# An encoder's MLP: pairs of up-projection tiles as seven products of blocks in place of eight

## The chip, the core and the metric

The kernel runs on one core of one Trainium2 chip. The metric is the device time of one execution in microseconds (us), as the median of several runs. The engines are named as in the profile: PE (TensorE; PEld is its weight load), DVE (VectorE), ACT (ScalarE), POOL (GpSimd) and SP (SyncE, which here only issues DMAs).

## What is computed

A bidirectional encoder of two layers, width 1024, runs over a prompt of 512 tokens and a sample of 256 with the same weights, 768 tokens in all. Each layer is an attention block with four kinds of heads and then this MLP:

```
def conv_gated_mlp(x, w_up, b_up, conv_w, conv_b, w_down):
    h = x @ w_up + b_up                      # 1024 -> 5632
    hp = jnp.pad(h, ((0, 0), (CONV_W // 2, CONV_W // 2), (0, 0)))
    h = conv_w[0] * hp[:, :-2] + conv_w[1] * hp[:, 1:-1] + conv_w[2] * hp[:, 2:] + conv_b
    a, b = jnp.split(h, 2, axis=-1)
    return (jax.nn.silu(a) * b) @ w_down     # 2816 -> 1024

...
x = x + conv_gated_mlp(rms_norm(x, g_ffn[l]), w_up[l], b_up[l], conv_w[l], conv_b[l], w_down[l])
```

All inputs and outputs are float32.

## The kernel before, in words

Activations are kept transposed: eight tiles of 128 features by 768 tokens. TensorE takes a rounded format (fp32r), so every factor is split into a high part, which ACT copies, and a low part, which `lo` (line 147) subtracts on POOL or DVE. `acc3` (lines 174 to 184) makes each product from three matmuls: high by high (L180), high by low (L182), low by high (L183). A matmul takes a 128x128 block of weights and up to 512 token columns; the prompt and the sample go separately, with 512 and 256 columns.

`weights` (from line 154) loads a block of weights by SP's queue into `wraw` (two buffers), makes `wh` on ACT (L158) and `wl` in halves of 512 columns on POOL (L147). `wh` and `wl` have four buffers of 1024 columns each.

The MLP (`mlp`, from line 1117) goes over 22 feature tiles i. For each i, `up` computes columns i and 22 + i of the up projection: 8 x 3 matmuls with 512 columns into a `mm` bank of PSUM and 8 x 3 with 256 into a `pt` bank (two banks of each). ACT adds the bias and writes `hb` (L1140), where the prompt and the sample lie with zeros around them. `conv` is one pass on ACT (L1147) and two on DVE (L1149, L1150) over 769 columns. Then come silu on ACT (L1163), the product of the halves on DVE (L1164), and its split into `gh` (ACT, L1167) and `gl` (DVE). The down projection (`down`) takes chunks of 8, 7 and 7 feature tiles. It stands on PE behind the first up tiles of the next chunk: per chunk eight output tiles, each with the prompt into a `sc` bank (two) and the sample into the `o` bank (one), and DVE adds each result to x (L1196).

Every engine works its list in order. The tile framework decides that order when the program is built, and it also inserts the waits on buffers.

Of the kernel before, what the change touches and what calls it, by code (L numbers as in the profile page):

```python
# [9 lines left out]
F32 = mybir.dt.float32  # L10
# [17 lines left out]
CHUNKS = ((0, 8), (8, 15), (15, 22))  # L28
# [18 lines left out]
RING, TMP_BUFS, P_BUFS, PT_BUFS, GH_BUFS = 32, 3, 9, 2, 9  # L47
# [8 lines left out]
       "rbc": "d", "pl": "d", "cmb": "d"}  # L56
WHOLD, DHOLD = (1, 3), (6, 7)
# [25 lines left out]
def encoder(ctx: ExitStack, tc, a, y):  # L83
# [11 lines left out]
    con = cp.tile([P, NCON], F32, name="con")  # L95
# [58 lines left out]
    def weights(src, n):  # L154
        raw = load_weights(src, n)
# [6 lines left out]
        return h, l  # L162

    def small_weights(src, n):
        raw = wp.tile([P, 1024], F32, tag="wraw", bufs=2, name="uraw")
        nc.sync.dma_start(out=raw[:, :n], in_=src)
        h = wp.tile([P, 256], F32R, tag="uh", bufs=2, name="uh")
        l = wp.tile([P, 256], F32R, tag="ul", bufs=2, name="ul")
        act.activation(h[:, :n], raw[:, :n], AF.Copy)
        lo(eng("ul"), l[:, :n], raw[:, :n], h[:, :n])  # L170
        return h, l
# [103 lines left out]
    def attention(l, x, par, sm, xin, loads, ready):  # L275
        lam_init = 0.8 - 0.6 * math.exp(-0.3 * l)


# [49 lines left out]
        def new_v(nm):  # L328
            return new_v1(nm + "0") + new_v1(nm + "1")

# [168 lines left out]
        class AHead:  # L499
# [7 lines left out]
            def first(self, si):  # L507
# [7 lines left out]
                for i in range(nt):  # L515
                    k0, k1 = max(0, i - 1) * P, min(nt, i + 2) * P
                    w = k1 - k0
                    p = pq[:, i * n:(i + 1) * n] if si else p_tile()[:, :w]
                    u = k0 - (i - 1) * P
                    jobs.append((mms, off + i * P, off + k0, w, p, con[:, C_AT + u:C_AT + u + w]))  # L520
                    probs.append((p, k0, w))
# [120 lines left out]
        def b_rope_k(kr):  # L642
# [3 lines left out]
            kc = con[:, C_KC:C_KC + 128].rearrange("p (t d) -> p t d", t=4)  # L646
            ks = con[:, C_KS:C_KS + 128].rearrange("p (t d) -> p t d", t=4)
# [101 lines left out]
        class DHead:  # L749
# [7 lines left out]
            def first(self, si):  # L757
# [5 lines left out]
                for g in range(0, nt, 2):  # L763
                    jobs = []
                    for m in range(2):
                        for i in (g, g + 1):
                            u = 384 - i * P
                            p = pq[m][:, i * n:(i + 1) * n] if si else p_tile()
                            jobs.append(([(self.st["q", m], self.st["k", m])], off + i * P, off, n, p,
                                         con[:, C_DT + u:C_DT + u + n]))  # L770
# [206 lines left out]
        if not xin:  # L977
            nc.sync.dma_start(out=con[:, C_AT:], in_=a["con"][:, C_AT:])
# [139 lines left out]
    def mlp(l, x, par, mp, u, ready):  # L1118
# [8 lines left out]

        def up(col, si):
            if col not in tiles:
                tiles[col] = upw(col)  # L1130
                hb = mp.tile([P, T + 3], F32, tag="hb", bufs=3, name="hb")
                bufs[col] = hb
                for c in (0, TP + 1, T + 2):
                    pool.memset(hb[:, c:c + 1], 0.0)
# [8 lines left out]
        def conv(col):  # L1143
            hb = bufs[col]
            t = mp.tile([P, T + 1], F32, tag="cv", bufs=4, name="cv")
# [9 lines left out]
        seq += [(c, si) for i in range(2, FT) for c in (i, FT + i) for si in (0, 1)]  # L1155

        def ff(i):
            while seq and not (i in tiles and FT + i in tiles and (i, 0) not in seq and (i, 1) not in seq
                               and (FT + i, 0) not in seq and (FT + i, 1) not in seq):
                up(*seq.pop(0))  # L1160
            ta = conv(i)
# [3 lines left out]
            gh = mp.tile([P, T], F32R, tag="gh", bufs=GH_BUFS, name="gh")  # L1165
            gl = slot("gl")
            act.activation(gh[:, :TP], ta[:, :TP], AF.Copy)  # L1167
            act.activation(gh[:, TP:], ta[:, TP + 1:], AF.Copy)
            lo(dve, gl[:, :TP], ta[:, :TP], gh[:, :TP])
            lo(dve, gl[:, TP:], ta[:, TP + 1:], gh[:, TP:])  # L1170
            return gh, gl

        def down(gs, f0, f1):
            last = f1 == FT
            order = [(m, si) for m in range(KT) for si in (0, 1)]
            if last:
                a0, b0 = (1, 0) if l < L - 1 else (0, 1)
                order = [(m, si) for m in range(5) for si in (0, 1)]
                order += [(m, si) for si in (a0, b0) for m in (5, 6, 7)]
            ws, count = {}, [0]  # L1180
            nf = f1 - f0
            for m, si in order:
                if m not in ws:
                    ws[m] = weights(a["w_down"][l, m, :, f0 * P:f1 * P], nf * P)
# [5 lines left out]
                else:  # L1190
                    out = b_sc() if si == 0 else b_o()
                i = acc3(out[:, :n], [((wh[:, i * P:(i + 1) * P], wl[:, i * P:(i + 1) * P]),
                                       (gs[i][0][:, off:off + n], gs[i][1][:, off:off + n])) for i in range(nf)])
                if last and si == b0 and m in DHOLD:
                    behind(i, marks[DHOLD.index(m)])
                dve.tensor_tensor(x[m][:, off:off + n], out[:, :n], x[m][:, off:off + n], op=ALU.add)  # L1196
                if last:
                    xsquare(x, m, si)
                    if (m, si) == (KT - 1, a0):
                        nxt.extend(ready(x))  # L1200

        nxt = []
        pending = None
        for f0, f1 in CHUNKS:
            gs = []
            for i in range(f0, f1):
                gs.append(ff(i))
                if pending is not None:
                    down(*pending)
                    pending = None  # L1210
            pending = (gs, f0, f1)
# [162 lines left out]
```

## Time and profile before

| | |
|---|---|
| median of three runs | 1946.84 us (1944.7 to 1950.02) |
| the profiled execution, its own time | 1950.42 us |
| its span, first to last instruction | 1948.5 us |
| granted TensorE clock, mean | 0.983 |
| PE / PEld busy | 96% / 84% of the span |
| DVE / ACT / POOL busy | 54% / 47% / 38% |
| first layer's MLP | about 433 to 950 us |
| second layer's MLP | about 1400 to 1948 us |

The profile gives for each engine its busy time, for each group of instructions its count, mean duration and the idle time of its engine ahead of it, and for each instruction its start. Matmuls are pipelined: a matmul's duration is longer than the distance to the next one's start, and that distance is what the engine spends on it.

### The profile page before, as it was taken

The page shows a single profiled execution, that of the slowest core. Times are in us where ns is not written, and L with a number is a line of the kernel's source. Part 1 is how long each engine was busy: PE and PEld are TensorE (multiplying, and loading weights), DVE is VectorE, ACT ScalarE, POOL GpSimd, SP SyncE. Part 2 cuts the span into 40 slices and gives each one's busy share as a digit, 9 for nine tenths or more (in the row PEclk, how much of TensorE's full clock was granted, in tenths as well). Part 3 has the DMA queues.
Part 4 walks back from the last instruction along what each step waited for, and adds up shares of the span by engine and source line. Part 5 has one row for each costly group of instructions (what it writes and reads, how often), then busy time and mean ns, then how long its engine had stood idle before and what let it go on. Part 6 is the DMA issues. An engine that isn't in the chain of part 4 may idle for free.

```text
span 1948.5 us, 28713 instructions
## 1 busy us (share of the span) xinstructions
PE 1876.7 (96%) x10932; PEld 1636.4 (84%) x10932; DVE 1042.9 (54%) x1875; ACT 914.7 (47%) x1776; POOL 736.1 (38%) x937
## 2 busy tenths in 40 slices
PE   8899998999999999999999999999999999999997
PEld 6778886888888888888978888778888888888886
DVE  5688779746442244134356877894554314432443
ACT  4466667545442244144335766773454314422441
POOL 1325536354333233333343363643543333323331
PEclk8899999999999999999999999999999999999998
DMA  4322005021222222221334110141122221122211
GB/s 171 91 62 75 26 12 147 26 73 56 71 57 64 66 65 58 63 67 59 115 96 127 50 43 17 47 122 54 56 75 65 65 65 58 58 69 66 63 57 65
DMA packets 46297, 133.64 MB, mean 69 GB/s; under 512 B 6736, under 2 KB 10704, under 8 KB 46160
## 3 DMA queue, kind: packets, MB, share of 16 engines
q1 hardware_dynamic: 45872, 131.56, 23.0%
q8 instruction: 86, 1.41, 0.3%
q14 instruction: 51, 0.42, 0.1%
q10 hardware_dynamic: 288, 0.26, 0.0%
HBM read 109.77 MB, written 6.29 MB: 60 GB/s over the span
## 4 chain that ended last, share of the span: by engine, by line
PE 82%; DVE 9%; ACT 3%; POOL 2%; issue 1%; DMA 1%; SPq 0%; DVEq 0%; ACTq 0%; POOLq 0%
PE mm L180 14%; PE mm L182 13%; PE mm L183 13%; PE pt L182 6%; PE pt L183 6%; PE pt L180 6%; PE sc L180 4%; PE sc L183 3%; PE sc L182 3%; PE sc L399 2%; PE o L378 2%; PE pt L370 2%; PE o L183 1%; PE o L180 1%; PE o L182 1%
## 5 line engine op out<-in xcount | busy, mean ns | idle before, releaser
L147 POOL TENSOR_TENSOR wl<-wraw,wh 128x512 fp32r<-128x512 f32 (+3 forms) x377 | 477.2, 1288 | 611.3 <-ACT wh L158 556.7
L158 ACT ACTIVATE wh<-wraw 128x1024 fp32r<-128x1024 f32 (+3 forms) x188 | 190.7, 1015 | 373.3 <-PE o L183 110.8
L1149 DVE SCALAR_TENSOR_TENSOR cv<-hb,par,cv 128x769 f32<-128x769 f32 x88 | 161.0, 1831 | 358.7 <-ACT cv L1147 358.7
L182 PE MATMUL mm<-ul,wh 128*128 128x512 f32 x704 | 275.2, 391 | 0.7 <-POOL ul L147 0.4
L180 PE MATMUL mm<-uh,wh 128*128 128x512 f32 x704 | 274.1, 391 | 0.1
L183 PE MATMUL mm<-uh,wl 128*128 128x512 f32 x704 | 273.9, 389 | 0.0
L182 PE MATMUL pt<-ul,wh 128*128 128x256 f32 x704 | 200.5, 285 | 1.5 <-POOL ul L147 1.4
L180 PE MATMUL pt<-uh,wh 128*128 128x256 f32 x704 | 199.8, 284 | 1.7 <-ACT wh L158 1.0
L183 PE MATMUL pt<-uh,wl 128*128 128x256 f32 x704 | 199.7, 284 | 0.0
L343 POOL TENSOR_SCALAR p<-p,s 128x512 f32<-128x512 f32 (+2 forms) x160 | 103.2, 659 | 217.9 <-DVE s L772 103.4
L183 PEld LDWEIGHTS mm<-uh,wl 128*128 128x128 f32 x704 | 132.2, 188 | 28.1
L182 PEld LDWEIGHTS mm<-ul,wh 128*128 128x128 f32 x704 | 132.5, 188 | 25.9 <-POOL ul L147 0.8
L180 PEld LDWEIGHTS mm<-uh,wh 128*128 128x128 f32 x704 | 132.3, 188 | 25.8 <-ACT hb L1140 0.6
L180 PEld LDWEIGHTS pt<-uh,wh 128*128 128x128 f32 x704 | 135.3, 192 | 6.2 <-ACT wh L158 1.8
L182 PEld LDWEIGHTS pt<-ul,wh 128*128 128x128 f32 x704 | 135.5, 192 | 5.8 <-POOL ul L147 1.9
L183 PEld LDWEIGHTS pt<-uh,wl 128*128 128x128 f32 x704 | 135.5, 192 | 0.2
L180 PE MATMUL mm<-xh,wh 128*128 128x256 f32 (+1 forms) x360 | 126.2, 353 | 2.3 <-DVE dl L147 1.7
L182 PE MATMUL mm<-xl,wh 128*128 128x256 f32 (+1 forms) x360 | 125.4, 349 | 0.9 <-DVE xl L147 0.9
L183 PE MATMUL mm<-xh,wl 128*128 128x256 f32 (+1 forms) x360 | 125.3, 349 | 0.0
L180 PE MATMUL sc<-gh,wh 128*128 128x512 f32 (+1 forms) x324 | 122.9, 379 | 0.0
L183 PE MATMUL sc<-gh,wl 128*128 128x512 f32 (+1 forms) x324 | 122.2, 377 | 0.0
L182 PE MATMUL sc<-gl,wh 128*128 128x512 f32 (+1 forms) x324 | 121.4, 375 | 0.0
(299 smaller groups left out, 4470.2 us busy)
## 6 DMA issues: line engine op xcount, KB each, us to landing
wraw<-w_up SPq DMA_DIRECT2D x88, 512.0 KB, 3.6
wraw<-w_down SPq DMA_DIRECT2D x32, 448.0 KB, 3.3
wraw<-w_in SPq DMA_DIRECT2D x26, 512.0 KB, 3.7
wraw<-w_down SPq DMA_DIRECT2D x16, 512.0 KB, 3.6
wraw<-w_o SPq DMA_DIRECT2D x16, 384.0 KB, 3.3
dk<-dh SPq DMA_DIRECT2D x32, 96.0 KB, 2.2
dq<-dh SPq DMA_DIRECT2D x32, 96.0 KB, 2.2
x<-x SPq DMA_DIRECT2D x8, 384.0 KB, 4.5
```

The source lines that it names most:

```text
L147: return eng.tensor_tensor(out, src, hi.bitcast(F32), op=ALU.subtract)
L158: act.activation(h[:, :n], raw[:, :n], AF.Copy)
L180: m = pe.matmul(out, ah, bh, start=i == 0, stop=False)
L182: pe.matmul(out, ah, bl, start=False, stop=False)
L183: pe.matmul(out, al, bh, start=False, stop=i == len(terms) - 1)
L343: e.tensor_scalar(t, t, r, 1.0, op0=ALU.mult, op1=ALU.mult)
L370: pe.transpose(pt[:, e * P:(e + 1) * P], probs[i][0][:, c:c + P], ident)
L378: pe.matmul(o[:, b:e], lhs, part[:, b - c0:e - c0], start=kt == 0 and q == 0, stop=kt == nt - 1 and q == 1)
L399: pe.matmul(out, q[:, q0:q0 + P], k[:, k0:k0 + n], start=i == 0, stop=i == len(mms) - 1)
L1149: dve.scalar_tensor_tensor(t, hb[:, 0:T + 1], par[:, w:w + 1], t, op0=ALU.mult, op1=ALU.add)
```

## The change

Feature tiles 0 to 3 (`PLAIN`) are computed as before. Tiles 4 to 21 are taken as pairs. For a pair the weights of columns i and 22 + i form a 2x2 matrix of blocks (column by half of the 1024 inputs), and the tokens another (half of the inputs by 384 tokens). Their product is formed by the Winograd form of Strassen's method: `up_pair` makes seven block products, each of 4 x 3 matmuls with 384 columns, alternately in `mm` and `pt` banks, and DVE adds them up (lines 1276 to 1300 of the changed kernel) straight into `hb`; only the first product leaves PSUM by ACT.

The factors have to be added up first. `token_sums` forms, once per layer and beside tiles 0 to 3, four sums of the tokens and splits them again. `pair_weights` forms four sums of the weights for each pair on DVE (L1248), and splits seven halves of 512 columns: `wh` on ACT (L1253), `wl` six times on DVE and once on POOL. The weights of a pair are prepared while the pair ahead of it is multiplied.

To make room and to keep the groups short, the down projection now takes chunks of 2, 4, 4, 4, 4 and 4 tiles and loads two output tiles' weights at once; raw weights have two more buffers (`uraw`); `gh`, `gl` and `cv` have fewer; the zeros in `hb` are written once per layer; and the attention masks leave the constant tile and are loaded once per layer. The last chunk's order of output tiles is changed as well.

```diff
-CHUNKS = ((0, 8), (8, 15), (15, 22))
+CHUNKS = ((0, 2), (2, 6), (6, 10), (10, 14), (14, 18), (18, 22))
+
+PLAIN, HF, PREP_M = 4, 384, 1
+ORDER, PREP_FIRST, TOK, URAW, CV = 1, 0, (0, 1, 3), 2, 3
...
+       "rbc": "d", "pl": "d", "cmb": "d", "ws": "dd", "wm": "ddddpdd", "tk": "d", "ts": "dddddddp", "tl": "ddd"}
...
+        msk = sm.tile([P, NCON - C_AT], F32, tag="msk", bufs=1, name="msk")
...
+        def token_sums():
...
+            for k in half:
...
+                for t, j in ((ta, k), (tb, k + 4)):
+                    eng("tk").tensor_tensor(t, xh[j].bitcast(F32), xl[j].bitcast(F32), op=ALU.add)
+
+                for out, p, q in ((first[k], ta[:, H1], ta[:, H0]), (ta[:, H0], tb[:, H1], ta[:, H1]),
+                                  (ta[:, H1], tb[:, H1], first[k]), (tb[:, H0], tb[:, H0], ta[:, H1])):
+                    eng("ts").tensor_tensor(out, p, q, op=ALU.subtract)
+                for nm, t in (("T2", ta[:, H1]), ("T3", ta[:, H0]), ("T4", tb[:, H0])):
...
+                    part(nm, k, t, *blocks[nm][k])
+                yield
...
+        def pair_weights(i, after=None):
+
+            r1, r2 = raw_tile(), raw_tile()
+            nc.sync.dma_start(out=r1, in_=a["w_up"][l, i])
+            nc.sync.dma_start(out=r2, in_=a["w_up"][l, FT + i])
+            raw = {"A11": r1[:, :512], "A12": r1[:, 512:], "A22": r2[:, 512:]}
...
+            for nm, p, q, op in (("S1", r2[:, :512], r2[:, 512:], ALU.add), ("S2", "S1", r1[:, :512], ALU.subtract),
+                                 ("S4", r1[:, 512:], "S2", ALU.subtract),
+                                 ("S3", r1[:, :512], r2[:, :512], ALU.subtract)):
...
+                j = eng("ws").tensor_tensor(raw[nm], p, q, op=op)
...
+            for nm, (h, lw) in w.items():
+                act.activation(h, raw[nm], AF.Copy)
+                lo(eng("wm"), lw, raw[nm], h)
+            return w
+
+        def up_pair(i):
...
+            def product(out, wn, bn):
+                h, lw = w[wn]
+                for k, (bh, bl) in enumerate(blocks[bn]):
+                    sl = slice(k * P, (k + 1) * P)
+                    pe.matmul(out, h[:, sl], bh, start=k == 0, stop=False)
+                    pe.matmul(out, h[:, sl], bl, start=False, stop=False)
+                    pe.matmul(out, lw[:, sl], bh, start=False, stop=k == KT // 2 - 1)
+                return out
...
+            p1, u2, u3, u4 = v[:, H0], v[:, H1], u[:, H0], u[:, H1]
+            act.activation(p1, product(out(), "A11", "B11"), AF.Copy)
+            dve.tensor_tensor(u2, product(out(), "S2", "T2"), p1, op=ALU.add)
...
+                plus(hb[0][:, 1:1 + HF], product(out(), "A12", "B21"), b1, p1)
+                dve.tensor_tensor(u3, product(out(), "S3", "T3"), u2, op=ALU.add)
+                p5 = product(out(), "S1", "T1")
+                dve.tensor_tensor(u4, p5, u2, op=ALU.add)
+                second(hb[1], p5, b2, u3)
+            second(hb[0], product(out(), "S4", "B22"), b1, u4)
+            plus(hb[1][:, 1:1 + HF], product(out(), "A22", "T4"), b2, u3)
...
             for i in range(f0, f1):
-                gs.append(ff(i))
+                ups(i)
+                after = None
                 if pending is not None:
-                    down(*pending)
+                    after = down(*pending)
                     pending = None
...
+                gs.append(gate(i))
+                if not PREP_FIRST and PLAIN <= i + 1 < FT:
+                    ready_w[i + 1] = pair_weights(i + 1, after)
```

In the built programs, DVE's list in the middle of the first layer's MLP read like this before. It is the end of one feature tile, and nothing else stands between it and the next tile's `conv`:

```order
L1149 SCALAR_TENSOR_TENSOR cv<-hb,par,cv 128x769
L1150 SCALAR_TENSOR_TENSOR cv<-hb,par,cv 128x769
L1164 TENSOR_TENSOR cv<-cv 128x769
L147 TENSOR_TENSOR gl<-cv,gh 128x512
L147 TENSOR_TENSOR gl<-cv,gh 128x256
```

In the changed program, twelve instructions of DVE's list from the middle of a pair that has no down projection beside it. Here `s` and `sraw` are sums of weights for the next pair, `u` and `hb` take products out of PSUM, `wl` is a low part, and `gl` belongs to the pair before:

```order
L150 TENSOR_TENSOR wl<-wraw,wh 128x512
L1298 TENSOR_TENSOR u<-pt,v 128x384
L1248 TENSOR_TENSOR s_6726<-uraw 128x512
L150 TENSOR_TENSOR gl<-cv,gh 128x769
L1300 TENSOR_TENSOR u<-mm,v 128x384
L1276 SCALAR_TENSOR_TENSOR hb_4943<-mm,par,u 128x128
L1276 SCALAR_TENSOR_TENSOR hb_4943<-mm,par,u 128x256
L1248 TENSOR_TENSOR sraw<-s_6726,wraw 128x512
L1248 TENSOR_TENSOR sraw<-wraw,uraw 128x512
L1276 SCALAR_TENSOR_TENSOR hb_4942<-pt,par,u 128x128
L1276 SCALAR_TENSOR_TENSOR hb_4942<-pt,par,u 128x256
L1248 TENSOR_TENSOR s_6730<-wraw,sraw 128x512
```

DVE now stands between PE and itself several times per pair: its list mixes the emptying of PSUM with the next pair's weights and the last pair's gate.

On PE, the change puts the first pair of a chunk among the previous chunk's down projection. Seven instructions of PE's list there (`T` and `uh`, `ul` are token blocks, `gh`, `gl` the gated activations):

```order
L1271 MATMUL pt<-T_5551,wl 128x384
L1269 MATMUL mm<-uh_4743,wh 128x384
L1270 MATMUL mm<-ul_4751,wh 128x384
L1271 MATMUL mm<-uh_4743,wl 128x384
L176 MATMUL o<-gh,wh 128x256
L178 MATMUL o<-gl,wh 128x256
L179 MATMUL o<-gh,wl 128x256
```

So of the pairs of a layer those that open a chunk are multiplied beside a down projection, and the others follow each other without one.

## Rows read from the trace of the kernel before

**Rows 1.** The page: its engines, and the chain that ended last, by engine

```profile
PE 1876.7 (96%) x10932; PEld 1636.4 (84%) x10932; DVE 1042.9 (54%) x1875; ACT 914.7 (47%) x1776; POOL 736.1 (38%) x937
...
PE 82%; DVE 9%; ACT 3%; POOL 2%; issue 1%; DMA 1%; SPq 0%; DVEq 0%; ACTq 0%; POOLq 0%
```

**Rows 2.** Busy time by engine in the MLP's stretches: start:end, length, busy, clock, DMA

```profile
433.00:950.00 517.00, 515.36 (x2955) 453.85 (x2954) 208.85 (x228) 204.88 (x282) 172.83 (x256) 1.00 0.22 65
1400.00:1948.00 548.00, 536.51 (x3065) 472.19 (x3063) 212.42 (x232) 202.19 (x277) 175.00 (x258) 0.99 0.21 64
```

**Rows 3.** Groups on PE: busy, mean ns | idle of PE ahead of them

```profile
L180 PE MATMUL mm<-uh,wh 128*128 128x512 f32 x704 | 274.1, 391 | 0.1
L180 PE MATMUL pt<-uh,wh 128*128 128x256 f32 x704 | 199.8, 284 | 1.7 <-ACT wh L158 1.0 <-DVE x L1062 0.7
```

**Rows 4.** Timeline of DVE, 730 to 800 us: start, duration, [idle before, releaser]

```profile
757.34 1.64 DVE L1149 SCALAR_TENSOR_TENSOR cv<-hb,par,cv 128x769 f32<-128x769 f32 x1 [5.57 <-ACT cv L1147]
759.09 1.02 DVE L1150 SCALAR_TENSOR_TENSOR cv<-hb,par,cv 128x769 f32<-128x769 f32 x1
...
774.02 1.64 DVE L1149 SCALAR_TENSOR_TENSOR cv<-hb,par,cv 128x769 f32<-128x769 f32 x1 [5.58 <-ACT cv L1147]
```

**Rows 5.** Timeline of PE, 512 columns, first and last of 24 in one product

```profile
604.60 0.40 PE L180 MATMUL sc<-gh,wh 128*128 128x512 f32 x1
...
609.87 0.39 PE L183 MATMUL sc<-gh,wl 128*128 128x512 f32 x1
```

**Rows 6.** Timeline of PE, 288 columns, first and last of 15 in a row

```profile
98.79 0.30 PE L182 MATMUL mm<-wl,xh 128*128 128x288 f32 x1
...
100.65 0.29 PE L180 MATMUL mm<-wh,xh 128*128 128x288 f32 x1
```

**Rows 7.** Groups on DVE by shape: busy, mean ns | idle before

```profile
L1149 DVE SCALAR_TENSOR_TENSOR cv<-hb,par,cv 128x769 f32<-128x769 f32 x88 | 161.0, 1831 | 358.7 <-ACT cv L1147 358.7
L1150 DVE SCALAR_TENSOR_TENSOR cv<-hb,par,cv 128x769 f32<-128x769 f32 x88 | 91.7, 1044 | 8.9 <-DVE cv L1149 0.5
L1164 DVE TENSOR_TENSOR cv<-cv 128x769 f32<-128x769 f32 x44 | 43.0, 978 | 3.5 <-ACT cv L1163 2.2
L147 DVE TENSOR_TENSOR gl<-cv,gh 128x512 fp32r<-128x512 f32 x44 | 30.4, 691 | 25.9 <-ACT gh L1167 25.9
L1196 DVE TENSOR_TENSOR x<-sc,x 128x512 f32<-128x512 f32 x38 | 26.2, 691 | 136.4 <-PE sc L183 136.4
L258 DVE SCALAR_TENSOR_TENSOR xt<-x,par,sc 128x512 f32<-128x512 f32 x32 | 22.3, 738 | 8.5 <-PE sc L220 8.4
L147 DVE TENSOR_TENSOR gl<-cv,gh 128x256 fp32r<-128x256 f32 x44 | 18.4, 418 | 0.0
L258 DVE SCALAR_TENSOR_TENSOR xt<-x,par,sc 128x256 f32<-128x256 f32 x32 | 14.2, 474 | 2.1 <-PE sc L220 1.8
L1196 DVE TENSOR_TENSOR x<-o,x 128x256 f32<-128x256 f32 x32 | 13.6, 425 | 70.4 <-PE o L183 70.4
```

**Rows 8.** Timeline of DVE, 8 to 62 us: two low parts in a row; one beside POOL

```profile
36.83 1.28 DVE L147 TENSOR_TENSOR wl<-wraw,wh 128x512 fp32r<-128x512 f32 x2
...
56.24 1.67 DVE L147 TENSOR_TENSOR dl<-dx,dh 128x512 fp32r<-128x512 f32 x1
```

**Rows 9.** Timeline of POOL around the same moment

```profile
54.63 2.73 POOL L147 TENSOR_TENSOR wl<-wraw,wh 128x512 fp32r<-128x512 f32 x2 [1.35 <-ACT xh L264]
```

**Rows 10.** Timeline of POOL in the first layer's MLP

```profile
755.90 2.27 POOL L147 TENSOR_TENSOR wl<-wraw,wh 128x512 fp32r<-128x512 f32 x2 [3.85 <-ACT wh L158]
```

**Rows 11.** Groups on ACT by shape: busy, mean ns | idle before

```profile
L1147 ACT ACTIVATE cv<-hb,par 128x769 f32<-128x769 f32 x88 | 90.7, 1033 | 6.8
L1163 ACT ACTIVATE cv<-cv 128x769 f32<-128x769 f32 x44 | 37.3, 848 | 127.0 <-DVE cv L1150 127.0
L1167 ACT ACTIVATE gh<-cv 128x512 fp32r<-128x512 f32 x44 | 27.8, 631 | 40.9 <-DVE cv L1164 40.9
```

**Rows 12.** DMA issues of the page: KB each, median us to landing

```profile
wraw<-w_up SPq DMA_DIRECT2D x88, 512.0 KB, 3.6
wraw<-w_down SPq DMA_DIRECT2D x32, 448.0 KB, 3.3
```

More of the change, by code (lines that the diff above doesn't have):

```diff
@@ L977, in attention @@
         if not xin:
-            nc.sync.dma_start(out=con[:, C_AT:], in_=a["con"][:, C_AT:])
+            load_masks()
         if l:
@@ L1126, in mlp, with next_hb @@
         tiles, bufs = {}, {}
+        hbs = [mp.tile([P, T + 3], F32, name=f"hb{j}") for j in range(3)]
+        for t in hbs:
+            for c in (0, TP + 1, T + 2):
+                pool.memset(t[:, c:c + 1], 0.0)
+        def next_hb():
+            hbs.append(hbs.pop(0))
+            return hbs[-1]
         def up(col, si):
@@ L1130, in up @@
                 tiles[col] = upw(col)
[L1131 to L1134, printed above, removed]
+                bufs[col] = next_hb()
             w, hb = tiles[col], bufs[col]
@@ new lines, in last_sums, with raw_tile, half_tile @@
+        def last_sums(first, part):
+            for k, t in enumerate(first):
+                part("T1", k, t, *blocks["T1"][k])
+        spare = []
+        ready_w = {}
+        stash = []
+        raws = [0]
+        def raw_tile():
+            raws[0] += 1
+            pool_, nm = (wp, "wraw") if raws[0] % (3 if URAW == 1 else 2) else (mp, "uraw")
+            return pool_.tile([P, 1024], F32, tag=nm, bufs=2 if nm == "wraw" else URAW, name=nm)
+        def half_tile():
+            if not spare:
+                h = wp.tile([P, 1024], F32R, tag="wh", name="wh")
+                lw = wp.tile([P, 1024], F32R, tag="wl", name="wl")
+                spare.extend([(h[:, :512], lw[:, :512]), (h[:, 512:], lw[:, 512:])])
+            return spare.pop(0)
@@ L1160, in ff, with gate @@
                 up(*seq.pop(0))
+        def gate(i):
             ta = conv(i)
@@ L1192, in down @@
                 i = acc3(out[:, :n], [((wh[:, i * P:(i + 1) * P], wl[:, i * P:(i + 1) * P]),
[L1193 to L1196, printed above, removed]
+                                       (gs[i][0][:, off + si:off + si + n], gs[i][1][:, off + si:off + si + n]))
+                                      for i in range(nf)])
+                if last and si == b0 and m in DHOLD[l]:
+                    behind(i, marks[DHOLD[l].index(m)])
+                i = dve.tensor_tensor(x[m][:, off:off + n], out[:, :n], x[m][:, off:off + n], op=ALU.add)
+                if (m, si) == (PREP_M, 1):
+                    mark = i
                 if last:
@@ L1206, in mlp @@
             for i in range(f0, f1):
-                gs.append(ff(i))
+                ups(i)
+                after = None
                 if pending is not None:
-                    down(*pending)
+                    after = down(*pending)
                     pending = None
+                if i == 0:
+                    steps = token_sums()
+                    stash.extend(next(steps))
+                if i < PLAIN:
+                    for _ in range(TOK[i] if i < len(TOK) else 0):
+                        next(steps)
+                if i == PLAIN - 1:
+                    last_sums(*stash)
+                if PREP_FIRST and PLAIN <= i + 1 < FT:
+                    ready_w[i + 1] = pair_weights(i + 1, after)
+                gs.append(gate(i))
+                if not PREP_FIRST and PLAIN <= i + 1 < FT:
+                    ready_w[i + 1] = pair_weights(i + 1, after)
             pending = (gs, f0, f1)
```

119 lines of the change are left out of this document (90 added, 29 removed).

## The prediction

> **What bounds the kernel now.** I read the page first. PE is busy 96% of the span and carries 82% of the chain that ended last, DVE 54% and 9% [rows 1]. A busy share is a mean over stages, so the windows of the two MLPs come next: PE is busy 515.4 of 517 us in the first and 536.5 of 548 in the second, at a granted clock of 1.00 and 0.99, which is the 2.4 GHz level. DVE has 209 and 212 us of work there, ACT about 205, POOL about 175 [rows 2]. Among the groups of instructions, 704 matmuls of each kind have between 0.1 and 1.7 us of idle time ahead of them in all [rows 3]. So the MLP is a row of matmuls without gaps. Time is gained there only by giving PE less to do, and it is lost as soon as another engine can't follow.
>
> What a matmul costs is the distance between starts. The convolution's first DVE pass runs once per column tile, and every second one of them stands 16.68 us apart: 757.34 and 774.02 [rows 4]. In these 16.68 us PE makes one feature tile, that is two columns of 24 matmuls with 512 columns and 24 with 256. One of each takes 0.3475 us together, 0.4525 ns per token column. A row of 24 with 512 columns alone goes at 5.27/23 = 0.229 us [rows 5], one of 288 columns at 1.86/14 = 0.133 us [rows 6]: 0.447 and 0.461 ns per column. The cost follows the columns with little besides.
>
> **What the change takes from PE.** A pair was 96 matmuls in 16.68 us. It becomes 7 products of 12 matmuls with 384 columns. No row has 384. By the mean of 512 and 256 it is 0.174 us, by the two ends above 0.172 and 0.177. A pair then takes 84 x 0.174 = 14.6 us (14.4 to 14.9) and saves 2.06 (1.8 to 2.3). There are 18 pairs in each of two layers, so PE is relieved of 36 x 2.06 = **74 us** (65 to 82). The four plain tiles and the down projection keep their matmuls. I take the mean, since 384 lies midway between shapes that both run in the same stretch.
>
> **What it puts on DVE.** Two low parts in a row take 1.28 us where one takes 0.69 [rows 7, 8], so independent instructions overlap by 0.09, and I charge each its mean duration less 0.09. Shapes that no row has lie between or beyond two that are there. Per pair, down projection aside:
> - four weight sums and six low parts of 512: 10 x 0.60 = 6.0
> - three sums out of PSUM of 384, between the 418 and 691 ns of 256 and 512: 3 x 0.46 = 1.4
> - the bias passes into `hb`, by the rows of L258 (474 and 738 ns): two of 384 at 0.52, two of 256 at 0.38, two of 128 at 0.25, together 2.3
> - the gate: four convolution passes at the 1044 ns of L1150, 3.8; the product and the low part of 769, 2 x 0.89 = 1.8
>
> That is **15.3 us** per pair [rows 7], against 14.6 of PE. Before, it was the gate alone, 5.6 us in 16.7. To it comes one low part on POOL, 2.27/2 = 1.13 us [rows 10]. What POOL does to DVE the rows show: a low part of 512 that takes 0.69 alone took 1.67 from 56.24 [rows 8], while POOL ran two of its own from 54.63 to 57.36 [rows 9]; it ended 0.55 after POOL. The same is in the convolution, whose first pass (beside POOL's `wl`) has a mean of 1831 ns and whose second has 1044 [rows 7]. So a POOL low part can stop DVE for nothing or for all of its 1.13 us, and the lone pair's DVE time lies between 15.3 and 16.4: it falls behind PE by 0.7 to 1.8 us. The Trainium skill (SBUF — State Buffer, Who interferes with whom) says that a DVE instruction with two SBUF inputs and a GpSimd instruction that reads SBUF exclude each other, and whoever comes first keeps the port for its whole instruction. By that rule the upper end would hold each time; the two rows agree with it.
>
> Over a whole chunk of four pairs DVE isn't the bound. PE needs 4 x 14.6 plus 8 x 4 x 3 x 0.3475 = 33.4 for the down projection, 91.8 in all. DVE needs 4 x 15.3 plus eight times 0.60 and 0.335 for adding to x [rows 7], 68.7, and 82 with every POOL low part (12 per chunk) counted in full. The trouble is the order: only the pair that opens a chunk (tiles 6, 10, 14, 18) lies beside a down projection, the other 14 per layer follow each other, 28 in all. What DVE is late in them PE loses, except what two things absorb: there are four PSUM banks for the products, so PE can run about two products, 4 us, ahead of DVE; and the gate of a lone stretch's last pair can wait for the down projection. Bounds per lone pair are therefore 0 and 1.8. I take **0.8**, just over what DVE's list alone gives, because the slack is about what POOL adds: 28 x 0.8 = **22 us** lost.
>
> **The other parts.** Token sums, per layer on DVE: 8 sums of 768 at 0.89, 14 of 384 and 16 low parts of 384 at 0.46, 21 us. They lie beside four plain tiles and the first small down projection, 4 x 16.68 + 16.7 = 83 us of PE. DVE has there also four gates (22), the x additions (7.5), the norm of the prompt (8) and the first pair's weights (6), 65 in all, and up to 20 POOL low parts, 23 us, can stop it: 88 against 83. So 0 to 5 us per layer; I take 4, near the end at which DVE has no room, **8 us** together. The 48 + 48 more additions to x are 45 us of DVE in all; they are in the chunk's sum, and the down projection covers them. If it didn't, PE would wait in the single `o` bank. ACT gets seven copies of 512 at 0.63, one eviction at about 0.6, two convolution passes at 1.03 and two of 0.85 per pair [rows 11]: 8.8 us of 14.6, no bound. SP loads as many bytes as before in fewer, larger pieces (512 KB land in 3.6 us [rows 12]), with two buffers more: nothing, covered by a pair's 14.6 us. The masks are loaded once more in the second layer, 0.79 MB, about 5.5 us by the same row: 0 to 5.5, and I take 0, since the list of SP has it behind the weights that the first projections need. POOL's zeros in `hb` go: it was idle anyway. The last chunk's tail is as before.
>
> **The sum.** -74 + 22 + 8 = -44 from the profiled execution's own 1950.4 (1.9 more than its span): 1906. That execution is 3.6 over the median of the runs, so I forecast 1903 for the median. No change is what lies within 0.3%, 5.8 us, of 1946.8; a measurement of this kernel can hardly tell less.
>
> **Rivals.**
> - *Everything is covered.* The lone pairs' DVE work spreads into the down projections and PE never waits: 1950.4 - 74 - 3.6 = 1873. For it speaks the chunk's sum (82 of 91.8), against it the order, in which the next pair's weights and the last gate stand between the evictions. 0.14.
> - *POOL's low part stops DVE in full each time.* 28 x 1.8 + 10 = 60 us are lost: 1933. For it speak rows 7 to 9, against it the slack of the banks. This is the mechanism of the rule named above. 0.18.
> - *Slower: DVE paces the lone pairs at full durations.* In its list the sums, low parts and bias passes of a pair depend on each other and on ACT's copies, so the overlap of 0.09 may be gone. At full means a pair is 17.5 us, with the POOL part 18.6 [rows 7, 10]: 4.0 over PE, 28 x 4.0 = 112, plus 8, less 74: 46 us more, 1993. The place is the first PSUM eviction of a pair, which stands behind the weights of the next. It decides against the change from 14.6 + (74 - 8)/28 = 17.0 us per lone pair on. Against it speaks that the list alternates the three kinds of work, so that neighbours are mostly independent. 0.11.
> - *The change doesn't save columns.* If a matmul of 384 cost what one of 512 does, 0.229, a pair would take 19.2, and 36 x 2.56 = 92 more: 2039. The 288-column row speaks against it. 0.02.
>
> The forecast has 0.55, with a range of its own from 1885 to 1921. The range from 1870 to 1937 takes in the first two rivals and leaves out the last two. Faster by over 0.3% are the forecast, full cover and nearly all of the second rival: 0.85. Within it 0.04, from the tail of the second and the beginning of the third; slower 0.11.
>
> **What would show it.** In the profile after: matmuls of 384 columns at 0.174 us apart; PE busy about 74 us less outright; DVE busy near 15 us of every lone pair, and the idle time of PE between pairs put down to DVE (`v`, `u`, `hb`) or to the `wl` of the next pair; no such idle time beside the down projections; beside POOL's low parts DVE's of 512 at over 1 us. The prediction is wrong if PE waits beside the down projections too, if lone pairs are more than 17 us apart, or if ACT or a DMA is what PE waits for.

## The result, and the profile after

| | before | after |
|---|---|---|
| median of the timed runs | 1945.77 us (1943.86 to 1950.02, 4 runs) | 1887.03 us (1884.93 to 1889.63, 4 runs) |
| profiled execution, own time | 1950.4 us | 1884.93 us |
| its span | 1948.5 us | 1883.0 us |

The ratio is 0.9696, 95% interval 0.9673 to 0.9719: faster, by about 59 us. The forecast was 1903 us, the range 1870 to 1937. Some 6 of the 65.5 us between the two spans lie ahead of the first MLP, which no step of the change explains: PE's first up projection begins at 427.2 us, before at 433.0, and the granted clock of the first 50 us was 0.90 after and 0.83 before. In the runs below, whose work ahead of it is that of the change, it begins anywhere from 424.4 to 433.3. The medians don't rest on these two executions.

The page of the kernel after, its engines and its chain by engine, beside [rows 1]:

```profile
PE 1807.9 (96%) x10500; PEld 1634.6 (87%) x10500; DVE 1462.7 (78%) x2687; ACT 931.2 (49%) x1836; POOL 634.5 (34%) x579
...
PE 80%; DVE 11%; ACT 3%; DMA 2%; issue 2%; POOL 1%; SPq 1%; DVEq 0%; ACTq 0%; POOLq 0%
```

PE has 68.8 us less work, and its idle time in the span is about what it was (75.1 us of 1883.0, before 71.8 of 1948.5). DVE went from 54% to 78%. The work that the change put on DVE has hardly turned into waiting on PE.

Groups on PE of the kernel after, with their idle time ahead, beside [rows 3], and the start of a lone pair and of the next on PE's timeline, beside [rows 4]:

```profile
L1269 PE MATMUL mm<-uh,wh 128*128 128x384 f32 x432 | 145.2, 336 | 0.0
L176 PE MATMUL sc<-gh,wh 128*128 128x512 f32 x312 | 123.0, 394 | 1.2 <-ACT gh L1319 1.2
L179 PE MATMUL o<-gh,wl 128*128 128x256 f32 x288 | 81.7, 284 | 0.0
```

```profile
700.63 0.34 PE L1269 MATMUL mm<-uh,wh 128*128 128x384 f32 x1
...
715.26 0.34 PE L1269 MATMUL mm<-uh,wh 128*128 128x384 f32 x1
```

The two starts are 14.63 us apart and belong to neighbouring pairs: 84 matmuls at 0.174 us, with no gap. Over all 3024 matmuls of products, 1512 in each layer, the mean distance to the next start is 0.1744 us and the longest 0.185. So PE waited in none of them.

The busy time of one chunk of four pairs, split where the work of PE splits. In the first stretch the down projection runs (between it PE makes one pair's worth of products), in the second there are products alone. The columns are start:end, length, busy time of PE, PEld, DVE, ACT and POOL with instructions, granted clock, DMA share, GB/s:

```profile
742.40:792.20 49.80, 49.80 (x286) 45.70 (x285) 34.27 (x56) 13.90 (x20) 8.68 (x7) 1.00 0.21 64
792.20:834.70 42.50, 42.50 (x246) 42.50 (x245) 41.60 (x62) 22.46 (x33) 10.37 (x6) 1.00 0.26 75
```

The whole chunk takes 92.3 us (the prediction's sum gave 91.8). PE is busy in all of it. DVE has 75.9 us of work (the prediction had 68.7 with no hindrance from POOL, 82 with all of it): in the second stretch, called the lone stretch below, it has 0.9 us free of 42.5, beside the down projection 15.5 of 49.8.

DVE's timeline in the lone stretch ahead of this (700 to 742 us; DVE's durations repeat in the next one), from the first to the third `v` (the sum of a pair's second product), which is once per pair, and three PE starts around the third:

```profile
705.90 0.55 DVE L1289 TENSOR_TENSOR v<-pt,v 128x384 f32<-128x384 f32 x1
...
721.13 0.55 DVE L1289 TENSOR_TENSOR v<-pt,v 128x384 f32<-128x384 f32 x1
...
741.43 0.54 DVE L1289 TENSOR_TENSOR v<-pt,v 128x384 f32<-128x384 f32 x1
```

```profile
737.88 0.33 PE L1270 MATMUL pt<-T,wh 128*128 128x384 f32 x1
738.06 0.33 PE L1271 MATMUL pt<-T,wl 128*128 128x384 f32 x1
...
743.81 0.34 PE L1269 MATMUL pt<-uh,wh 128*128 128x384 f32 x1
```

The first two sums are 15.23 us apart, with DVE idle for 0.77 us between them. PE moves on by 14.63, so DVE falls behind. The third sum, in the last pair of that stretch, starts 3.0 us after the last matmul of its product, which began at 738.06. It ends at 741.97, and PE needs that `pt` bank again only at 743.81, 1.8 us later. No product of this chunk, read in this way buffer by buffer, waits longer for its first reader. In the two lone pairs ahead the longest was 1.4 and 1.2 us, and in the pair beside the down projection 0.9; the shortest time from a last read to PE's next matmul in that bank was 1.1 us.

### The profile page after: what moved, and what is told of

It is laid out like the page before. It is cut to its first block, busy times and chain, and to the rows that moved or that the text cites. A ratio compares the mean times of both kernels' runs of the same rounds, so it can differ in the third digit from the quotient of the medians.

```text
span 1883.0 us, 28393 instructions
## 1 busy us (share of the span) xinstructions
PE 1807.9 (96%) x10500; PEld 1634.6 (87%) x10500; DVE 1462.7 (78%) x2687; ACT 931.2 (49%) x1836; POOL 634.5 (34%) x579
## 4 chain that ended last, share of the span: by engine, by line
PE 80%; DVE 11%; ACT 3%; DMA 2%; issue 2%; POOL 1%; SPq 1%; DVEq 0%; ACTq 0%; POOLq 0%
PE mm L176 7%; PE mm L178 7%; PE mm L179 6%; PE mm L1269 5%; PE mm L1271 5%; PE mm L1270 5%; PE pt L1270 4%; PE pt L1269 4%; PE pt L1271 4%; PE sc L178 4%; PE sc L176 4%; PE sc L179 4%; PE sc L412 2%; PE o L179 2%; PE o L176 2%; PE o L178 2%
## 5 line engine op out<-in xcount | busy, mean ns | idle before, releaser
L150 POOL TENSOR_TENSOR wl<-wraw,wh 128x512 fp32r<-128x512 f32 (+2 forms) x181 | 254.6, 1429 | 194.3 <-ACT wh L163 140.6
L1269 PE MATMUL mm<-uh,wh 128*128 128x384 f32 x432 | 145.2, 336 | 0.0
L1270 PE MATMUL mm<-ul,wh 128*128 128x384 f32 x432 | 144.9, 335 | 0.0
L1271 PE MATMUL mm<-uh,wl 128*128 128x384 f32 x432 | 144.9, 335 | 0.0
L163 ACT ACTIVATE wh<-wraw 128x1024 fp32r<-128x1024 f32 (+4 forms) x92 | 90.6, 987 | 100.9 <-PE mm L178 48.3
L150 DVE TENSOR_TENSOR pl<-pt,ph 128x512 fp32r<-128x512 f32 (+2 forms) x160 | 101.4, 644 | 31.3 <-ACT ph L362 30.1
L1253 ACT ACTIVATE wh<-wraw 128x512 fp32r<-128x512 f32 x72 | 45.2, 628 | 153.7 <-PE o L179 92.3
L460 ACT ACTIVATE p<-p,nm 128x512 f32<-128x512 f32 (+2 forms) x144 | 86.9, 606 | 44.0 <-DVE nm L455 21.7
L362 ACT ACTIVATE ph<-pt 128x512 fp32r<-128x512 f32 (+2 forms) x160 | 86.4, 563 | 32.5 <-PE o L403 12.7
L452 DVE CUSTOM_DVE_ANT_0 p<-sc,msk 128x512 f32<-128x512 f32 (+2 forms) x144 | 78.1, 552 | 29.8 <-PE sc L412 23.9
L1270 PE MATMUL pt<-T,wh 128*128 128x384 f32 x288 | 96.3, 334 | 0.0
L1269 PE MATMUL pt<-T,wh 128*128 128x384 f32 x288 | 96.2, 334 | 0.0
```

Source lines behind the costliest of these rows:

```text
L150: return eng.tensor_tensor(out, src, hi.bitcast(F32), op=ALU.subtract)
L460: act.activation(p, p, AF.Exp, bias=nm[:, i:i + 1], scale=escale, accum_out=s[:, i:i + 1])
L1269: pe.matmul(out, h[:, sl], bh, start=k == 0, stop=False)
L1270: pe.matmul(out, h[:, sl], bl, start=False, stop=False)
L1271: pe.matmul(out, lw[:, sl], bh, start=False, stop=k == KT // 2 - 1)
```

## The experiments

Differences from the change are worked out from the ratios to the kernel before (ratio less 0.9696, times 1946 us). With intervals of about 0.002 on either side of each ratio, such a difference is known to some 6 us. All edits are edits of the changed kernel.

| run | median us | ratio, 95% interval | against the change |
|---|---|---|---|
| e1_all_plain | 1956.68 | 1.0047 [1.0027, 1.0067] | +68 |
| e2_load1 | 1900.64 | 0.9747 [0.9728, 0.9766] | +10 |
| e2_load3 | 1948.18 | 1.0001 [0.9985, 1.0017] | +59 |
| e3_one_tag | 1916.63 | 0.9844 [0.9827, 0.9861] | +29 |
| e4_pinned | 1906.79 | 0.9782 [0.9761, 0.9804] | +17 |
| e5_plain3 | 1913.61 | 0.9829 [0.9808, 0.9850] | +26 |
| e7_no_pool | 1895.93 | 0.9741 [0.9718, 0.9765] | +9 |
| e7_pool2 | 1906.71 | 0.9804 [0.9774, 0.9833] | +21 |
| e8_less | 1880.14 | 0.9669 [0.9653, 0.9686] | -5 |
| e9_no_sums | 1883.33 | 0.9679 [0.9663, 0.9694] | -3 |
| e10_order0 | 1891.61 | 0.9724 [0.9710, 0.9738] | +5 |
| e10_prep3 | 1885.26 | 0.9703 [0.9687, 0.9718] | +1 |

**Everything but the products.** All tiles are plain and the token sums go. Smaller chunks, masks, buffers and loads stay as in the change, and so does what is computed.

```
-PLAIN, HF, PREP_M = 4, 384, 1
+PLAIN, HF, PREP_M = 22, 384, 1
...
-                if i == 0:
-                    steps = token_sums()
...
-                if i == PLAIN - 1:
-                    last_sums(*stash)
```

> All of the change but the products: every feature tile is computed as before, no sums of tokens or weights; the chunks of 2 and 4, the raw buffers, the masks and the new order of the last chunk stay. If the seven products alone bring the gain and the rest costs what the longer distances between the down projection's matmuls show (about 2 to 3 us per layer), this is 5 us over the kernel before: about 1951, 64 over the change. If the rest of the change brings part of the gain, it is below 1940. If the smaller chunks are what kept the change from its 74 us, it is 1955 to 1960.

It is 0.47% slower than the kernel before, 9 us (5 to 13), between the first and the last of the three readings, and the products with their sums bring 68. The prediction had set the whole rest at nothing. From the two traces: from the first matmul of an up projection to the last of its down projection, 556.0 us became 560.2 in the first layer and 559.0 became 561.1 in the second. The second attention went from 387.5 to 389.8, but it takes from 387.2 to 390.8 in the other runs, so this tells little. About 2 us per layer of the MLPs' part are the down projection's matmuls: 512 columns stand 0.2317 and 0.2314 us apart in place of 0.2297 and 0.2293, 256 columns 0.121 in place of 0.119. Where these 2 ns per matmul come from (shorter groups, or more banks handed over) wasn't separated.

**More DVE work per pair.** The weight sum S3 is formed once or three times more, with the same result: 0.60 or 1.80 us of DVE per pair, 36 pairs. The edit of the second run (the first has 1 in place of 3):

```
                 j = eng("ws").tensor_tensor(raw[nm], p, q, op=op)
+                for _ in range(3 if nm == "S3" else 0):
+                    dve.tensor_tensor(raw[nm], p, q, op=op)
```

> One more DVE instruction of 128x512 (0.60 us) in every pair's weight sums. Theory A (DVE is late in the pairs without a down projection, but by at most 3.4 us, and 1.1 us of slack are left before PE waits for a bank): lateness grows by 0.6 in each of two such pairs in a row, the slack is just used up: 0 to 5 us over the change, 1887 to 1892. Theory B (what DVE has over PE's 14.6 us in such a pair is paid by PE at once, as the prediction had it): 18 to 28 pairs at 0.6: 11 to 17 us, 1898 to 1904. Theory C (DVE has real room in these pairs, its list is shorter there): no change.

> Three more such DVE instructions (1.8 us) per pair. Theory A: 3.6 us of lateness over two pairs against 1.1 of slack, 2.5 lost per chunk and more in the pair after: 20 to 40 us, 1907 to 1927. Theory B: 1.8 in 18 to 28 pairs, 32 to 50 us, 1919 to 1937. Theory C: below 8 us.

One repeat, 22 us of added work, cost 10. That lies between Theory A's 5 and Theory B's 11 (the median, 1900.64, is in B's range), so this run doesn't decide between them. By the page DVE's busy time rose by more than the repeats, from 1462.7 to 1504.3: other instructions got longer too (the `wl<-uraw` low parts have a mean of 865 ns in place of 683). The new waits of PE are short ones, at ACT's copy of a pair's first product and at a low part of the weights:

```profile
PE mm L1271 <- ACT v L1290: 2.7, 8, 0.7
...
PE mm L1273 <- DVE wl L150: 1.6, 6, 0.3
```

Three repeats, 65 us (62.2 by the page), cost 59, beyond both readings. So there is a little room, and behind it the loss is about as large as the added work. The same two stretches of a chunk with three repeats, first the products alone, then the down projection, and the wait that is new:

```profile
715.00:763.90 48.90, 43.01 (x234) 41.73 (x233) 46.02 (x72) 22.92 (x35) 6.13 (x5) 0.97 0.19 61
763.90:816.60 52.70, 52.25 (x298) 47.80 (x298) 36.40 (x58) 13.10 (x19) 11.53 (x8) 1.00 0.20 65
```

```profile
PE mm L1271 <- DVE hb L1278: 22.1, 8, 3.9
```

The chunk is 101.6 us long, 9.3 more. The lone stretch alone has 5.9 us of idle PE. The wait (us in total, times, longest) comes 8 times: a product waits for its `mm` bank, which DVE's second bias pass still reads. That is the wait that the prediction had put into the changed kernel; there it has no row.

Not all of the 59 us is this waiting. In the products of the change the granted clock is 1.00 throughout; with three repeats it falls to 0.50, the 1.2 GHz level, in some 27 us among them, each time during a wait of PE of 2.2 to 3.9 us or within 2 us of its end. A stretch of the second MLP in the change, and one of the first with three repeats, behind such a wait (the clock is the third number from the end):

```profile
1380.00:1860.00 480.00, 480.00 (x2719) 452.33 (x2718) 400.40 (x603) 202.09 (x294) 112.81 (x70) 1.00 0.21 65
```

```profile
850.00:855.00 5.00, 5.00 (x17) 5.00 (x17) 5.00 (x7) 3.41 (x5) 1.70 (x1) 0.50 0.00 0
```

Half of the 27 us, some 13 of the 59, is an estimate of what the lower clock cost.

**Two banks in place of four.** All products go through the two `mm` banks.

```
             def out():
-                return (b_mm, b_pt)[next(turns) % 2]()[:, :HF]
+                return b_mm()[:, :HF]
```

> All seven products of a pair go through the two mm banks, in place of two mm and two pt banks. DVE empties a product up to 3.4 us after its end in the change. With four banks PE meets a bank again after two other products (6.3 us from one end to the next start in it), with two after none: a product may be left for about 2.1 us. If the banks are what absorbs DVE's lateness, PE waits in the pairs where it exceeds 1.5 us, mostly the one that opens the down projection and the first of a layer: 1 to 3 us per chunk, 10 to 30 us over the change (1897 to 1917). If DVE's lateness is harmless for another reason, within 4 us of the change.

```profile
PE mm L1269 <- DVE hb L1276: 9.0, 22, 1.8
```

29 us are lost, within the 10 to 30 expected. Lone pairs stand 15.4 to 15.7 us apart in place of 14.63, about what DVE's own list takes (15.4). Matmuls of products stand 0.181 us apart on average in place of 0.174, with the waits counted in; over 3024 of them that is some 20 us, 9 of them this wait. With the same DVE work and half the banks, DVE's lateness reaches PE. In this trace PE's list also has another order (the fourth product is no longer split around the third), so not all 29 us need be the banks'. (The expectation miscounts: between two uses of a bank stand two to four other products with four banks, and one with two.)

**A longer stretch without a down projection.** The first product of the pair after a down projection is held behind the last matmul of that projection.

```
+                    first = pe.matmul(out, h[:, sl], bh, start=k == 0, stop=False)
+                    if final:
+                        behind(first, final.pop())
...
+                final[:] = [i]
...
+        final = []
```

> The second pair of a chunk is held on PE behind the last product of the down projection, so that the down projection no longer reaches into it and three pairs follow each other alone instead of two. Theory A: DVE's lateness has a third pair to grow in, 0.6 to 1.8 us more against 1.1 of slack: 0 to 2 us in each of eight chunks, and PE waits once at the single bank of the sample products, which stand in a row: 5 to 20 us over the change. If the spreading of the down projection does not matter: within 3 us of the change.

Only the products in the `mm` banks were held: 24 of that pair's matmuls still ran among the down projection's. The down projection's stretch, then the products alone, and the new wait:

```profile
741.10:790.20 49.10, 47.03 (x265) 42.16 (x264) 31.55 (x43) 11.98 (x15) 14.85 (x9) 1.00 0.19 62
790.20:836.20 46.00, 46.00 (x267) 46.00 (x266) 45.56 (x74) 24.64 (x37) 7.72 (x5) 1.00 0.27 80
```

```profile
PE o L176 <- DVE x L1358: 9.8, 16, 0.7
```

The lone stretch grew from 42.5 to 46.0 us, and PE lost nothing in it, with DVE down to 0.44 us of room. The 17 us went in the down projection: its last three groups now follow each other in the single `o` bank with nothing between, and PE waits for the additions to x. The prediction's remark that PE would wait there if it lost its cover is the case here. In the change itself, products stand between these groups.

**POOL's share of the low parts.** None of a pair's seven low parts on POOL, or two in place of one.

```
-"wm": "ddddpdd"
+"wm": "d"
...
+"wm": "ddpdpdd"
```

> All seven low parts of a pair on DVE, none on POOL: 0.60 us more for DVE, one POOL instruction (1.13 us alone, 1.64 in the mean of the change) less to stop it. If POOL's low part costs DVE nothing, this is the same as the run with one more DVE instruction: 10 us over the change. If it stops DVE for its whole time, DVE gains 0.5 to 1 us per pair, and since PE has no gaps left there the time stays: within 3 us of the change. Half of it: 0 to 5 us over.

> Two of the seven low parts on POOL, five on DVE: 0.60 us less for DVE, one more POOL instruction of 1.13 to 1.64 us to stop it. If POOL stops DVE in full, DVE has 0.5 to 1 us more per pair, as with one more DVE instruction or worse: 8 to 18 us over the change. If POOL costs DVE nothing: no change, since PE has no gaps left to close.

Both lose, 9 and 21 us, and at the same place. By the expectations the first speaks for a POOL part that costs DVE nothing, and the second for one that stops it in full, so the times alone don't settle it. The wait for the `sc` bank of the down projection, first without POOL, then with two on POOL:

```profile
PE sc L176 <- DVE x L1355: 9.4, 6, 1.6
```

```profile
PE sc L176 <- DVE x L1355: 14.3, 6, 2.4
```

It comes once in each of three chunks per layer, where the down projection begins. In the change this wait doesn't occur, though DVE ends the lone stretch 3.0 us late there too. In the first run DVE has one low part more to do, 36 in all, 22 us, and its busy time rises by 4.8 (1462.7 to 1467.5). So the part on POOL had cost it some 17 us, about 0.5 us per pair (an estimate from these two figures). In the second run it has 36 parts less, and its busy time rises by 22.7, to 1485.4: the second part on POOL costs DVE more than it takes off. The wait makes up 9.4 us in the first run and 14.3 of 21 in the second; the rest of the second wasn't followed.

**Three plain tiles in place of four.**

```
-PLAIN, HF, PREP_M = 4, 384, 1
+PLAIN, HF, PREP_M = 3, 384, 1
```

> Three plain feature tiles in place of four, so 19 pairs per layer by seven products. PE is relieved of 2 x 2.03 = 4 us more. The sums of the tokens then lie beside three tiles and the small down projection, 67 us of PE, where DVE has 60 us of work and POOL's low parts can stop it for up to 18. If POOL stops DVE for half of that or less: 4 us under the change, about 1883. If in full: up to 11 us per layer lost, 1887 to 1905.

```profile
PE mm L1269 <- ACT wh L1253: 8.9, 4, 3.9
```

One more pair per layer should save 2.05 us, and the run is 26 slower, beyond the 1905 that was expected at the worst. It is lost where the layer begins. The first pair's weights come behind the token sums and the gates on DVE and ACT, and the largest new wait of PE is for the copies of those weights. In the stretch from 433 to 560 us PE is busy 118.1 of 127 us, at a granted clock of 0.97.

**Less DVE work.** The third tap of the convolution is left out in the 18 feature tiles of each layer that are made as seven products.

```
-            dve.scalar_tensor_tensor(t, hb[:, 2:T + 3], par[:, w + 2:w + 3], t, op0=ALU.mult, op1=ALU.add)
+            if col % FT < PLAIN:
+                dve.scalar_tensor_tensor(t, hb[:, 2:T + 3], par[:, w + 2:w + 3], t, op0=ALU.mult, op1=ALU.add)
```

> The change, with the third tap of the convolution left out in the 18 feature tiles of each layer that are made as seven products (the output then isn't the reference's). It takes two DVE instructions of 1.17 us out of each pair, 36 x 2.33 = 84 us of DVE in all, and nothing of PE. Theory A (DVE is full in the lone pairs of the change, but its lateness is absorbed by the four PSUM banks, so PE is hardly held up): gain 0 to 8 us against the change's 1887, that is 1879 to 1887. Rival B (DVE is the bound wherever it is full, as the dear added work of the runs with a repeated sum suggests): each us of DVE that is taken away also counts, at least half of it, gain 25 us or more, 1862 or less.

80 us of DVE are gone (1462.7 to 1382.2), and the time falls by 5 (the two intervals overlap), as Theory A has it. In 445 us of the second layer's MLP, first of the change, then of this run:

```profile
1380.00:1825.00 445.00, 445.00 (x2539) 421.48 (x2538) 374.62 (x570) 188.38 (x275) 96.34 (x61) 1.00 0.23 70
```

```profile
1380.00:1825.00 445.00, 445.00 (x2547) 422.62 (x2546) 339.11 (x541) 184.84 (x269) 90.61 (x62) 1.00 0.22 68
```

With 35.5 us of DVE less, PE is busy all the time in both, and does 8 matmuls more of 2540. So DVE costs the changed kernel next to nothing. It stands just at the point from which it would cost.

**No token sums.** The products read blocks of the plain tokens in place of the sums and differences.

```
-            blocks.update(T2=[], T3=[], T4=[])
...
+            blocks["T2"], blocks["T3"], blocks["T4"] = blocks["B21"], blocks["B11"], blocks["B22"]
...
-                    steps = token_sums()
-                    stash.extend(next(steps))
...
+                    token_sums()
```

> The change without the token sums: the three products that read T2, T3 and T4 read B21, B11 and B22 in their place and that of T1 reads the second half of the tokens as it is (the output then isn't the reference's); the 21 us of DVE per layer are gone, PE keeps all its matmuls. The prediction put the sums at 8 us (4 per layer): 1879. Theory A (the plain tiles and the first small down projection cover them, with four plain tiles just enough): 0 to 4 us, 1883 to 1887. Rival B (their DVE work stretches the plain tiles, whose 512-column matmuls were at 0.237 us in the change and at 0.229 before): 8 to 12 us, 1875 to 1879.

3 us less, within what the measurement can tell from nothing. The plain tiles and the first down projection cover the sums: in the change, DVE is busy 68.9 of the 81 us from 433 to 514.

**Two other orders.** The other order of the products in one run, and in the other the next pair's weights two row tiles of the down projection later.

```
-ORDER, PREP_FIRST, TOK, URAW, CV = 1, 0, (0, 1, 3), 2, 3
+ORDER, PREP_FIRST, TOK, URAW, CV = 0, 0, (0, 1, 3), 2, 3
...
-PLAIN, HF, PREP_M = 4, 384, 1
+PLAIN, HF, PREP_M = 4, 384, 3
```

> The change with its other order of the seven products (S1 T1 third and S3 T3 fourth, A12 B21 fifth; the switch ORDER is 0). The same matmuls and the same DVE work; the product that two sums read (P5) stands two products earlier and its bank is held by the later one of them while the next product runs. Theory A (four banks absorb what DVE is late): 1883 to 1892. Rival B (the bank of P5 is held until the second bias pass, DVE's order in the list then makes PE wait once per lone pair, 0.5 us or more each): 1900 or more.

> The change with the weights of the next pair put behind the x addition of the fourth row tile of the down projection, not of the second (PREP_M 3): DVE then empties the down projection's banks sooner, and the six low parts of the next pair come up to 8 us later. Theory A (the place of a loss is the pair that opens the down projection, and DVE is full from there on back to the first lone pair): the time moves by 5 us or less either way, unless the low parts come too late for the next pair's second product, when each chunk loses the up to 4 us that banks can't absorb, 8 chunks: up to 1919. A version that beats the change would show here, by 5 us at most.

The first is 5 us slower, at the upper end of its first reading and at the edge of what can be told. The second makes no difference: its two MLPs take 525.9 and 526.2 us from first to last matmul, those of the change 525.9 and 526.3. No run that computes the reference was faster than the change by more than the measurement can tell.

## Why the prediction was right, and where it was not

- *PE's matmuls set the time; fewer columns, less time.* Right. A matmul of 384 columns takes 0.1744 us where 0.174 was worked out, a pair 14.63 where 14.6 was. The up projection's time on PE fell from 370.6 to 334.3 and from 372.8 to 336.9 us, 72 together. The term was 74. By the times, the run without the products puts them at 68, all their costs included. The 4 us between lie inside the measurement.
- *DVE needs 15.3 us per pair.* Right: between the first two sums shown above it works for 14.46 of 15.23 us, with three of a pair's four convolution passes; with the fourth (0.93) that is 15.4. (Its 5.6 us for the gate before left out the hindrance that its own rows show: by the means of [rows 7] that gate takes 7.8.)
- *28 lone pairs lose 0.8 us each, 22 us.* This is the step that failed, and not by its count. The lone stretch of a chunk is 42.5 us, 2.9 pairs. Nor is a lateness of some 0.7 us per pair far off. It is the charge. The prediction itself says that the banks let PE run about 4 us ahead of DVE, and that the down projection gives DVE time back. Then only what exceeds that allowance within one chunk is lost: 2.9 x 0.8 = 2.3 us is less than 4, and DVE has 15.5 us of room in the next down projection. Measured: a lateness of 3.0 us at most in the chunk that was read, and 0.9 again beside its down projection; no matmul of a product over 0.185 us behind the one ahead, in either layer. The idle time of PE between pairs that the prediction named as its sign is missing. Taking 80 us of DVE work away brings some 5 us, and halving the banks costs 29. So the term was near 0, which is the first rival's mechanism.
- *POOL's low part stops DVE.* In the first two pairs of the lone stretch it hardly did, because of what it runs beside; in the third it did. Here are POOL's low parts at these places, and what DVE does there:

```profile
712.12 1.30 POOL L150 TENSOR_TENSOR wl<-s,wh 128x512 fp32r<-128x512 f32 x1 [12.35 <-ACT wh L1253]
729.59 2.61 POOL L150 TENSOR_TENSOR wl<-s,wh 128x512 fp32r<-128x512 f32 x1 [16.17 <-DVE hb L1276]
734.29 1.75 POOL L150 TENSOR_TENSOR wl<-wraw,wh 128x512 fp32r<-128x512 f32 x1 [2.09 <-ACT wh L163]
```

```profile
712.54 0.73 DVE L1276 SCALAR_TENSOR_TENSOR hb<-mm,par,u 128x128 f32<-128x128 f32 x2
...
731.49 1.86 DVE L150 TENSOR_TENSOR wl<-sraw,wh 128x512 fp32r<-128x512 f32 x2
...
734.80 1.78 DVE L150 TENSOR_TENSOR wl<-s,wh 128x512 fp32r<-128x512 f32 x1
...
737.04 1.52 DVE L1168 SCALAR_TENSOR_TENSOR cv<-hb,par,cv 128x769 f32<-128x769 f32 x1
738.47 3.03 DVE L1169 SCALAR_TENSOR_TENSOR cv<-hb,par,cv 128x769 f32<-128x769 f32 x2
```

  At 712.12 it lies beside sums that read a PSUM bank, and neither is slowed: 1.30 us on POOL, 0.73 for two passes on DVE. At 729.59 DVE had begun first and runs a row of low parts and weight sums, and POOL takes twice as long (2.61), while two of DVE's take 1.86 in place of 1.28. At 734.80, behind a POOL low part that began first, DVE's takes 1.78 in place of 0.68. The convolution passes behind it take 1.52 and 3.03, in place of 1.01 and 1.94, while POOL runs low parts of the down projection's weights. The Trainium skill (SBUF — State Buffer, Who interferes with whom) says that a DVE instruction with at most one SBUF input, outside the modes that use both ports, doesn't contend with GpSimd; that one with two SBUF inputs does with a GpSimd instruction that reads SBUF; and that whichever starts first keeps the port for its whole instruction. The trace agrees: 0.73 us unchanged at 712.54, 1.78 in place of 0.68 at 734.80. The prediction made a rival of that rule (1933) as if every POOL low part met a DVE instruction with two SBUF inputs, and as if PE then paid. The four rows of DVE from 731.49 on take 8.2 us in place of 4.9. That is more than the 1.8 by which its lateness grows there, from 1.2 to 3.0, and the banks took that too.
- *Token sums 8 us.* Too dear: 3 us without them, not to be told from 0. The prediction feared 88 us of DVE beside 83 of PE, and DVE was busy 68.9 of the 81 us read. That this hangs on the four plain tiles, the run with three shows.
- *All else nothing.* Too cheap: 9 us (5 to 13), from smaller chunks and what came with them. The traces show 6 of it in the MLPs; the masks' second load could not be told apart.
- *The slower rival: full durations, 17.5 us per pair.* It fell; independent instructions overlapped as in [rows 8]: low parts in a row start 0.60 us apart. Its break-even was 17.0 us per lone pair. Three repeats of a weight sum put DVE's list at 15.4 + 1.8 = 17.2, and that kernel takes the time of the one before (1.0001). That this comes so close is in part chance, since the lower clock is in that time.
- *Columns not saved.* It fell with the pace of 0.174.

In sum: -74 + 22 + 8 = -44 was forecast. By the runs it is about -68 for the products with DVE and token sums included, and +9 for the rest: -59. One charge was some 22 too high, the sums some 5, and one left out was 9: 18 in all, where the forecast was 15 us late; the 3 between lie inside the measurement. That 1887 fell within the forecast's own 1885 to 1921 is luck: without the 9 us that it left out, it would have been 1878.

## What to carry to other kernels

When an engine falls behind in one stretch and has room in the next, charge only the lateness that exceeds the buffers' allowance in one round, not the lateness times the number of steps. The change sits at the edge of that allowance: DVE could lose 80 us of work for some 5 us of gain, while 65 us more cost 59 (some 13 of them by the lower clock behind the waits), so a busy share of 78% tells neither side. Look at each stretch, and at which buffer is handed over when.

## What was not expected of the hardware

With the down projection cut into groups of four tiles, its matmuls of 512 columns stood 0.2315 us apart in place of 0.2295 in the run without products, over some 1050 of them; in the change, waits left out, it was 0.2307. And a POOL low part beside busy DVE low parts took 2.61 us where 1.30 was its time beside sums out of PSUM; the low part that stays on POOL in each pair has a mean of 1.64 us in the groups by shape. And in the run with three repeats the granted clock fell to 0.50 at waits of 2.2 to 3.9 us, so that a wait cost more than its own length.
